# Stick-breaking attention and HGRN2 on one core: new durations in a list schedule, the causal mask by a matmul, softplus's maximum by ScalarE

## The chip, the core and the metric

The kernel runs on one core of a Trainium2 chip. The metric is device time in microseconds (us), of one launch; the time of a kernel is the median of its runs. A core has TensorE (PE, matmuls, with weight loads shown apart as PEld), VectorE (DVE), ScalarE (ACT), GpSimd (POOL) and SyncE (SP, which issues DMAs). Each engine takes its instructions strictly in the order in which they are written for it, and waits on semaphores for the others.

## The reference

One decoder block on 1024 tokens of width 1024, in float32: a norm and a projection to 5632 columns, two branches (8 heads of stick-breaking attention, 4 heads of HGRN2), a gated merge, a projection, and a SwiGLU network. The change lies in the attention:

```python
def stick_breaking_attention(q, k, v):
    ...
        z = jnp.einsum('bhtd,bhsd->bhts', qb, kb).astype(jnp.float32) * scale
        ...
        causal = s_idx < t_idx
        sp = jnp.where(causal, jax.nn.softplus(z), 0.0)
        rest = lax.cumsum(sp, axis=3, reverse=True) - sp
        w = jnp.where(causal, jnp.exp(jax.nn.log_sigmoid(z) - rest), 0.0)
```

The kernel uses log_sigmoid(z) = z - softplus(z): the weight is exp(z - c), with c the running sum of softplus from the right, the own column included. Softplus is max(z, 0) + ln(1 + exp(-|z|)). Where a key is not in the past, z is set to -2^100, which makes softplus and weight 0.

## The kernel before

All float32 factors are split into a high and a low part in TensorE's own 32-bit format, so a product is two or three matmuls. The program has three parts: stage one (projections, both branches), stage two (merge and output projection), and the SwiGLU network with Strassen-Winograd products. Only stage one is touched.

**Stage one's order is made by a planner.** Functions such as `proj`, `scores`, `values` and `hgrn` don't issue instructions; they record operations through helpers that give each a duration: `A` (ScalarE), `V` (VectorE), `G` (GpSimd), `M` and `T` (matmuls and transposes on TensorE) and `L` (loads and stores on SyncE, each charged at least 0.47 us, or its KB / 350). `Plan.issue` then plays a list schedule. It keeps a clock, adds fixed delays between engines (2.0 us behind a DMA), takes at each moment, per engine, the ready operation with the longest way to the end, and writes the instructions in that order. Tiles are counted in rings: an operation that needs a new tile waits until one of its ring is free. What stands in the program is thus a fixed order for each engine; how long things really take only decides where an engine then waits. All these instructions are issued from one line of `Plan.issue`, so they all have line L180 in the profile, and are told apart by the names of their tiles.

**Names of tiles.** `pj`: accumulators of the projections (3 banks); they have the lowest rank (-1) and so fill TensorE's holes. The last of them are 16 gate projections that nothing in the stage waits for. `oh`, `ol`: high and low part of a weight (split by GpSimd and VectorE). `hq`, `lq`, `hk`, `lk`: queries and keys of two heads, both parts. `qs`, `ks`: the layout for one head, with one buffer each (`ks0`, `ks1` for the two parts); six DMAs fill them. `z`: scores (2 banks). `aa`, `ww`: tiles of the softplus chain. `th`, `tl`: parts of a tile that is to be multiplied. `vv`: values. `ms`: other matmul results (3 banks). `kb`, `dl`, `ql`, `tail`, `state`: HGRN2.

**The score chain** (`scores`, line 548 on). For each of 4 pairs of heads, each head of it and each block of 128 queries, the scores of 128 to 1024 keys are made in one or two tiles of up to 512 columns; 96 tiles in all, 64 of them with a diagonal block. For a tile: two matmuls (queries by `ks0`, by `ks1`) into a bank `z`; on the diagonal VectorE overwrites the future with `never` under the mask `future`; ScalarE makes |z|, Exp and Ln; VectorE adds max(z, 0), scans from the right, and subtracts the scan from `z`; ScalarE takes Exp. The bank comes free with the subtraction.

```python
V(stt, aw, zw, 0.0, aw, n=w, op0=ALU.max, op1=ALU.add)
V(nc.vector.tensor_tensor_scan, cw[:, ::-1], aw[:, ::-1], aw[:, ::-1],
  0.0 if prev is None else prev[:, 0:1], op0=ALU.add, op1=ALU.max, n=w,
  aps=prev is not None)
```

The scan computes state = max(a + state, a), which is a + state since both are at least 0. `values` (line 589) transposes the weights, splits them and multiplies by `vv`; `hgrn` (line 637) runs the other branch.

Of the kernel before, what the change touches and what calls it, by code (L numbers as in the profile page):

```python
# [19 lines left out]
P = 128  # L20
# [7 lines left out]
NEG = -float(2.0**100)  # L28
# [172 lines left out]
def hybrid_block(ctx: ExitStack, tc, xT, wi, wb, wo, wg, wu, wd, vec, outT):  # L201
    nc = tc.nc
# [46 lines left out]
    bones_r = const1.tile([P, P], F32R, name="bones_r")  # L249
    future = const1.tile([P, P], I8, name="future")  # L250
    never = const1.tile([P, P], F32, name="never")
    eps_t = const.tile([P, 1], F32, name="eps_t")
# [10 lines left out]
    def setup(sp):  # L263
        make_identity(nc, ident)
        t2 = sp.tile([P, P], F32, tag="t2", name="t2")
        nc.vector.memset(t2, 0.0)
        nc.vector.memset(t2[0:64, 0:64], 1.0)
        nc.vector.memset(t2[64:128, 64:128], 1.0)
        nc.vector.tensor_copy(bones_r, t2)
        nc.vector.memset(never, NEG)  # L270
        nc.gpsimd.memset(future, 1.0)
        nc.gpsimd.affine_select(
            out=future, in_=future, pattern=[[1, P]], compare_op=ALU.is_ge, fill=0.0,
            base=0, channel_multiplier=-1)
        nc.vector.tensor_scalar(qg, vt[:, V_Q:V_Q + 1], 0.125, None, op0=ALU.mult)
# [12 lines left out]
        nc.vector.tensor_scalar(omlb, lb, -1.0, 1.0, op0=ALU.mult, op1=ALU.add)  # L288
        nc.vector.tensor_scalar(nomlb, omlb, -1.0, None, op0=ALU.mult)
# [34 lines left out]
    pre.close()  # L324
    future = future.bitcast(U8)

# [37 lines left out]
    def V(fn, *args, n=HALF, aps=0, rank=0, part=False, holds=(), **kw):  # L364
        us = 0.07 + n / 960 + 0.061 * aps
        return plan.op("V", us, [(fn, args, kw)], rank, part=part, holds=holds)

    def G(fn, *args, us, rank=0, after=(), holds=(), **kw):
        return plan.op("G", us, [(fn, args, kw)], rank, after, holds=holds)

    def M(cols, mms, rank=0, after=(), holds=()):

        return plan.op("P", cols / 2400 + 0.003 * len(mms),
                       [(nc.tensor.matmul, m[:3], dict(start=m[3], stop=m[4])) for m in mms],
                       rank, after, holds=holds)

    def T(outs, after=(), holds=()):

        return plan.op("P", 0.11 * len(outs), [(nc.tensor.transpose, (o, i, ident), {})
                                               for o, i in outs], 0, after, holds=holds)  # L380
# [19 lines left out]
    def pool_copy(dst, src, rank=0, after=(), holds=()):  # L400
        return G(nc.gpsimd.tensor_scalar, dst, src, 1.0, 0.0, op0=ALU.mult, op1=ALU.add, us=0.6,
                 rank=rank, after=after, holds=holds)
# [38 lines left out]
    def take_x(h):  # L441
# [47 lines left out]
    def sums(out, src, w, n, after=()):  # L489

        hi, lo = new("th", dt=F32R)[:, :n], new("tl", dt=F32R)[:, :n]
        G(nc.gpsimd.tensor_scalar, hi, src, 1.0, 0.0, op0=ALU.mult, op1=ALU.add,
          us=0.05 + n / 930, holds=(lo,) if after else (lo, out))
        V(tt, lo, src, hi.bitcast(F32), op=ALU.subtract, n=n)
        return M(2 * n, [(out, w, hi, True, False), (out, w, lo, False, True)], after=after)
# [52 lines left out]
    def scores(j, last):  # L548
        d = heads[j]
        for e in range(2):  # L550
# [9 lines left out]
            for tb in range(8):  # L560
                n = (tb + 1) * P
                prev = None
                for c0, c1 in [(0, n)] if n <= 512 else [(512, n), (0, 512)]:
# [73 lines left out]
    def hgrn(hd, last):  # L637
# [5 lines left out]
        for h in range(2):  # L643
# [7 lines left out]
            pair = lambda t, m: t.rearrange("p (n u m) -> p n u m", u=2, m=m)  # L651
            G(nc.gpsimd.tensor_tensor, at, key, q, op=ALU.mult, us=1.15, after=(last,))
            dg = new("ms")
# [3 lines left out]
            for li, m in enumerate(LEVELS):  # L657
                nb = HALF // (2 * m)
                bv = pair(bb, m)
                if m == 1:  # L660
# [4 lines left out]
                    for t, u in ((key, 0), (q, 1)):  # L665
                        G(nc.gpsimd.tensor_tensor, ev, ev, pair(t, 1)[:, :, u, :], op=ALU.mult,
                          us=0.6)
                    lv = new("ms")
# [37 lines left out]
            ds_ = new("ms")  # L706
            M(2048, [(ds_[:, c], ktok[:, c], vtok[:, c], True, True) for c in cs])
            before = []
# [15 lines left out]
            o, sq = new("tail"), new("tail")  # L724
            d["free hi", h] = M(4096, mms, holds=(o, sq))
            A(nc.scalar.copy, o, op, ps=True)
# [393 lines left out]
```

## Time and profile before

| | us |
|---|---|
| median of 3 runs | 1580.96 (1579.17 to 1581.63) |
| the profiled execution's own time | 1582.63 |
| its span (first to last instruction) | 1580.9 |
| last matmul of stage one that is no projection | starts at 692.2 |
| first matmul of stage two | after 742.5 |

Over the span TensorE is busy for 1531.5 us (97%), VectorE for 1223.1 (77%), ScalarE for 751.6 (48%) and GpSimd for 215.3 (14%). A busy TensorE is not one at its peak: matmuls overlap, and the ends that the profile shows are modelled. In a row of the profile "aa<-z" means that `aa` is written and `z` read; "x96" is a count; behind the bar follow busy time, mean duration in ns, and the idle time of the engine just before, with what ended it. Waits are given as total, number of times and longest.

### The profile page before, as it was taken

The page shows a single profiled execution, that of the slowest core. Times are in us where ns is not written, and L with a number is a line of the kernel's source. Part 1 is how long each engine was busy: PE and PEld are TensorE (multiplying, and loading weights), DVE is VectorE, ACT ScalarE, POOL GpSimd, SP SyncE. Part 2 cuts the span into 40 slices and gives each one's busy share as a digit, 9 for nine tenths or more (in the row PEclk, how much of TensorE's full clock was granted, in tenths as well). Part 3 has the DMA queues.
Part 4 walks back from the last instruction along what each step waited for, and adds up shares of the span by engine and source line. Part 5 has one row for each costly group of instructions (what it writes and reads, how often), then busy time and mean ns, then how long its engine had stood idle before and what let it go on. Part 6 is the DMA issues. An engine that isn't in the chain of part 4 may idle for free.

```text
span 1580.9 us, 20533 instructions
## 1 busy us (share of the span) xinstructions
PE 1531.5 (97%) x7213; PEld 1249.6 (79%) x7213; DVE 1223.1 (77%) x2095; ACT 751.6 (48%) x1375; POOL 215.3 (14%) x231
## 2 busy tenths in 40 slices
PE   7999999999999999999999999999999999999999
PEld 5778887887778778888888878788888888778887
DVE  8798889999999776962657799888887777566553
ACT  5555767577657655452333363333333333244442
POOL 6121202301121000322441210000000000000000
PEclk9999999999999999999999999999999999999999
DMA  4303132113312232154334454666643333687672
GB/s 165 88 29 89 62 77 69 39 55 78 92 34 67 74 92 59 54 198 141 121 121 128 150 157 169 213 213 213 213 160 107 107 107 107 234 276 220 195 221 94
DMA packets 82247, 201.12 MB, mean 127 GB/s; under 512 B 9824, under 2 KB 11872, under 8 KB 80736
## 3 DMA queue, kind: packets, MB, share of 16 engines
q1 hardware_dynamic: 77536, 191.42, 38.5%
q10 hardware_dynamic: 4608, 8.39, 1.5%
q8 instruction: 57, 0.93, 0.3%
q14 instruction: 46, 0.38, 0.1%
HBM read 131.61 MB, written 55.57 MB: 118 GB/s over the span
## 4 chain that ended last, share of the span: by engine, by line
PE 71%; DVE 15%; DMA 5%; ACT 4%; issue 3%; SPq 1%; POOL 1%; DVEq 0%; ACTq 0%; POOLq 0%
PE f L908 25%; PE pj L180 16%; PE ms L180 6%; DVE aa L180 4%; PE f L1054 4%; PE f L1056 4%; PE f L1052 4%; PE pj L300 2%; PE pj L299 2%; PE pj L301 2%; DMA ks<-lk 2%; ACT aa L180 2%; PE z L180 2%; DMA rb<-act_d 1%; DVE ol L180 1%
## 5 line engine op out<-in xcount | busy, mean ns | idle before, releaser
L180 PE MATMUL pj<-ah,oh 128*128 128x512 f32 x704 | 288.9, 410 | 1.2 <-POOL oh L180 1.2
L180 PE MATMUL pj<-ah,ol 128*128 128x512 f32 x704 | 278.1, 395 | 0.4 <-DVE ol L180 0.4
L180 PE MATMUL pj<-al,oh 128*128 128x512 f32 x704 | 277.2, 394 | 0.0
L908 PE MATMUL f<-fh,oh 128*128 128x512 f32 x616 | 243.9, 396 | 3.2 <-ACT p L962 1.7
L908 PE MATMUL f<-fl,oh 128*128 128x512 f32 x616 | 243.5, 395 | 0.6 <-DVE fl L838 0.6
L908 PE MATMUL f<-fh,ol 128*128 128x512 f32 x616 | 243.2, 395 | 0.0
L235 ACT CAST oh<-w 128x512 fp32r<-128x512 f32 x168 | 102.4, 620 | 191.6 <-PE f L908 145.9
L180 PEld LDWEIGHTS pj<-ah,ol 128*128 128x128 f32 x704 | 133.5, 190 | 31.1 <-DVE ol L180 1.3
L180 PEld LDWEIGHTS pj<-ah,oh 128*128 128x128 f32 x704 | 134.3, 191 | 24.5 <-POOL oh L180 2.2
L180 PEld LDWEIGHTS pj<-al,oh 128*128 128x128 f32 x704 | 134.3, 191 | 22.3 <-issue 0.2
L236 DVE TENSOR_TENSOR ol<-w,oh 128x512 fp32r<-128x512 f32 x168 | 113.8, 684 | 37.7 <-ACT oh L235 37.4
L908 PEld LDWEIGHTS f<-fh,oh 128*128 128x128 f32 x616 | 115.5, 188 | 33.5 <-ACT p L962 2.2
L908 PEld LDWEIGHTS f<-fl,oh 128*128 128x128 f32 x616 | 115.5, 188 | 28.7 <-DVE fl L838 1.0
L908 PEld LDWEIGHTS f<-fh,ol 128*128 128x128 f32 x616 | 115.5, 188 | 28.1
L180 POOL TENSOR_SCALAR oh<-w 128x512 fp32r<-128x512 f32 x84 | 66.0, 787 | 396.2 <-PE pj L180 326.4
L1052 PE MATMUL f<-bh,ah 128*128 128x512 f32 x296 | 115.3, 393 | 4.0 <-ACT bh L235 4.0
L1054 PE MATMUL f<-bl,ah 128*128 128x512 f32 x296 | 117.5, 397 | 1.3 <-DVE bl L236 1.3
L1056 PE MATMUL f<-bh,al 128*128 128x512 f32 x296 | 117.3, 396 | 0.0
L236 DVE TENSOR_TENSOR al<-ra,ah 128x512 fp32r<-128x512 f32 x73 | 50.4, 690 | 73.1 <-ACT ah L235 72.9
L180 DVE TENSOR_TENSOR_SCAN aa<-aa 128x384 f32<-128x384 f32 (+3 forms) x96 | 95.1, 992 | 1.1
L235 ACT CAST ah<-ra 128x512 fp32r<-128x512 f32 x73 | 45.5, 623 | 102.8 <-PE f L1054 95.3
L180 DVE TENSOR_TENSOR ol<-w,oh 128x512 fp32r<-128x512 f32 x84 | 62.0, 739 | 18.7 <-POOL oh L180 18.1
(272 smaller groups left out, 3015.1 us busy)
## 6 DMA issues: line engine op xcount, KB each, us to landing
w<-wi SPq DMA_DIRECT2D x42, 512.0 KB, 3.6
rb<-act_d SPq DMA_DIRECT2D x73, 256.0 KB, 4.0
w<-wg SPq DMA_DIRECT2D x22, 512.0 KB, 3.8
w<-wu SPq DMA_DIRECT2D x22, 512.0 KB, 4.1
w<-wd SPq DMA_DIRECT2D x22, 512.0 KB, 6.7
wd_d<-ds SPq DMA_DIRECT2D x44, 256.0 KB, 5.2
act_d<-c SPq DMA_DIRECT2D x11, 1024.0 KB, 3.9
act_d<-bs SPq DMA_DIRECT2D x44, 256.0 KB, 3.3
```

The costliest lines, as they stand in the source:

```text
L180: fn(*[a.real() if isinstance(a, View) else a for a in args], **{k: v.real() if isinstance(v, View) else v for k, v in kw.items()})
L235: pin(nc.scalar.copy(hi, src))
L236: pin(nc.vector.tensor_tensor(lo, src, hi.bitcast(F32), op=ALU.subtract))
L299: nc.tensor.matmul(out, hi[:, ws], a[ka][0][:, hs(h)], start=first and i == 0, stop=False)
L300: nc.tensor.matmul(out, hi[:, ws], a[ka][1][:, hs(h)], start=False, stop=False)
L301: nc.tensor.matmul(out, lo[:, ws], a[ka][0][:, hs(h)], start=False, stop=last and i == n - 1)
L908: nc.tensor.matmul(out, a[i][:, ws], bl[k][j], start=start and k == 0 and i + j == 0, stop=k == 3 and i == 1, skip_group_check=True)
L1052: nc.tensor.matmul(bank[d], hi[:, ws], bh, start=first and p == 0, stop=False, skip_group_check=True)
L1054: nc.tensor.matmul(bank[d], hi[:, ws], bl, start=False, stop=False, skip_group_check=True)
L1056: nc.tensor.matmul(bank[d], lo[:, ws], bh, start=False, stop=p == NP - 1, skip_group_check=True)
```

## The change

Four edits, all in stage one:

1. Durations that the planner uses: a scan costs two passes instead of one; matmuls 2255 columns per us instead of 2400; transposes, GpSimd's operations and HGRN2's small matmuls get new figures. Loads (`L`) and the delays between engines stay.
2. The mask: `never` now holds -2^100 on and above the diagonal and 0 below, and a third matmul, identity by `never`, adds it to the diagonal block between the two score matmuls. VectorE's overwriting goes.
3. Softplus's maximum: ScalarE makes Relu(z) in a second tile (`ww`, later overwritten with the weights), and VectorE's addition goes.
4. The scan adds that tile: state = (a + state) + Relu(z).

```diff
-    future = const1.tile([P, P], I8, name="future")
-    never = const1.tile([P, P], F32, name="never")
+    never = const1.tile([P, P], F32R, name="never")
+    ident_r = const1.tile([P, P], F32R, name="ident_r")
...
     def V(fn, *args, n=HALF, aps=0, rank=0, part=False, holds=(), **kw):
-        us = 0.07 + n / 960 + 0.061 * aps
+        cycles = 2 * n if fn == nc.vector.tensor_tensor_scan else n
+        us = 0.067 + cycles / 960 + 0.061 * aps
...
-        return plan.op("P", cols / 2400 + 0.003 * len(mms),
+        return plan.op("P", us or cols / 2255 + 0.003 * len(mms),
...
-        return plan.op("P", 0.11 * len(outs), [(nc.tensor.transpose, (o, i, ident), {})
+        return plan.op("P", 0.11 * len(outs) - 0.08, [(nc.tensor.transpose, (o, i, ident), {})
...
-            G(nc.gpsimd.tensor_tensor, acc, acc, sq, op=ALU.add, us=1.15, after=(last_split[0],))
+            G(nc.gpsimd.tensor_tensor, acc, acc, sq, op=ALU.add, us=1.5, after=(last_split[0],))
...
-        M(2048 * 2, [(ss, ones, acc, True, True)])
+        M(2048, [(ss, ones, acc, True, True)])
...
-                    last = M(2 * w, mms, after=(last,))
                     if diag:
-                        V(nc.vector.copy_predicated, z[:, w - P:w], future, never, n=P)
+                        mms.insert(1, (z[:, w - P:w], ident_r, never, False, False))
+                    last = M(2 * w + P * diag, mms, after=(last,))
                     a, c, y = new("aa"), new("aa"), new("ww")
                     aw, cw, yw = a[:, :w], c[:, :w], y[:, :w]
                     A(act, aw, zw, AF.Abs, n=w, ps=True)
+                    A(act, yw, zw, AF.Relu, n=w, ps=True)
                     A(act, aw, aw, AF.Exp, n=w, scale=-1.0)
                     A(act, aw, aw, AF.Ln, n=w, aps=1, bias=one_t)
-                    V(stt, aw, zw, 0.0, aw, n=w, op0=ALU.max, op1=ALU.add)
-                    V(nc.vector.tensor_tensor_scan, cw[:, ::-1], aw[:, ::-1], aw[:, ::-1],
-                      0.0 if prev is None else prev[:, 0:1], op0=ALU.add, op1=ALU.max, n=w,
+                    V(nc.vector.tensor_tensor_scan, cw[:, ::-1], aw[:, ::-1], yw[:, ::-1],
+                      0.0 if prev is None else prev[:, 0:1], op0=ALU.add, op1=ALU.add, n=w,
                       aps=prev is not None)
...
-                last = M(8 * (n + 64), [(lv[:n, c * 64:(c + 1) * 64], dl[:, c * P:c * P + n],
+                last = M(0, [(lv[:n, c * 64:(c + 1) * 64], dl[:, c * P:c * P + n],
                                          ql[:, c * 64:(c + 1) * 64], True, True)
-                                        for c in range(4)], after=(last,))
+                                        for c in range(4)], after=(last,),
+                         us=0.43 + 0.003 * n)
```

The new durations move instructions all over the stage. The first place that matters later is on TensorE, between the two heads of the second pair, where queries and keys are loaded anew. `z` by the numbered `ks` are the last scores of the old head and, at the end, the first of the new one; before:

```order
L180 MATMUL z<-ks_2200,qs 128x512
L180 MATMUL z<-ks_2218,qs 128x512
L180 MATMUL pj<-ah_158,oh 128x512
...
L180 MATMUL ms<-th,ones_r 128x512
L180 MATMUL ms<-tl,ones_r 128x512
L180 MATMUL pj<-ah_148,oh 128x512
...
L180 MATMUL ms<-ql,dl 64x64 x4
L180 MATMUL z<-ks_2796,qs 128x128
L180 MATMUL z<-ks_2817,qs 128x128
```

and after the change:

```order
L180 MATMUL z<-ks_2288,qs 128x512
L180 MATMUL z<-ks_2309,qs 128x512
L180 MATMUL pj<-ah_162,oh 128x512
...
L180 MATMUL ms<-th,vv 128x256
L180 MATMUL ms<-tl,vv 128x256
...
L180 MATMUL z<-ks_2784,qs 128x128
L180 MATMUL z<-never,ident_r 128x128
L180 MATMUL z<-ks_2799,qs 128x128
```

Between the old head's last score matmul and the new head's first stood 36 projection matmuls, 2 wide and 4 narrow others; now there are 27 projection matmuls and 4 others of 256 columns. The mask matmul stands between the two of a tile.

The second place is VectorE's queue in the middle of the scores (the scan is shown as the other operations with three operands are: `aa<-aa` before, `aa<-aa,ww` now; `ww<-z,aa` is the subtraction that frees the bank). Before:

```order
L180 COPY_PREDICATED z<-future,never 128x128
L180 TENSOR_TENSOR ol<-w,oh 128x512
L180 SCALAR_TENSOR_TENSOR aa<-z,aa 128x512
L180 SCALAR_TENSOR_TENSOR aa<-aa 128x512
L180 SCALAR_TENSOR_TENSOR aa<-z,aa 128x128
L180 TENSOR_TENSOR tl<-ms,th 128x512
L180 SCALAR_TENSOR_TENSOR aa<-aa 128x128
L180 TENSOR_TENSOR ww<-z,aa 128x512
```

and after the change:

```order
L180 SCALAR_TENSOR_TENSOR aa<-aa,ww 128x512
L180 TENSOR_TENSOR ol<-w,oh 128x512
L180 SCALAR_TENSOR_TENSOR aa<-aa,ww 128x384
L180 TENSOR_TENSOR ww<-z,aa 128x512
L180 TENSOR_TENSOR tl<-ms,th 128x384
L180 TENSOR_TENSOR ww<-z,aa 128x384
```

A tile with a diagonal took four instructions here (overwrite, addition, scan, subtraction) and takes two.

More of the change, by code (lines that the diff above doesn't have):

```diff
@@ L269, in setup @@
         nc.vector.tensor_copy(bones_r, t2)
-        nc.vector.memset(never, NEG)
-        nc.gpsimd.memset(future, 1.0)
+        nc.vector.tensor_copy(ident_r, ident)
+        t3 = sp.tile([P, P], F32, tag="t3", name="t3")
+        nc.gpsimd.memset(t3, NEG)
         nc.gpsimd.affine_select(
-            out=future, in_=future, pattern=[[1, P]], compare_op=ALU.is_ge, fill=0.0,
+            out=t3, in_=t3, pattern=[[1, P]], compare_op=ALU.is_ge, fill=0.0,
             base=0, channel_multiplier=-1)
+        nc.vector.tensor_copy(never, t3)
         nc.vector.tensor_scalar(qg, vt[:, V_Q:V_Q + 1], 0.125, None, op0=ALU.mult)
@@ L324, in hybrid_block @@
     pre.close()
-    future = future.bitcast(U8)
     warm = pm()
@@ L369, in G, with M @@
         return plan.op("G", us, [(fn, args, kw)], rank, after, holds=holds)
-    def M(cols, mms, rank=0, after=(), holds=()):
-        return plan.op("P", cols / 2400 + 0.003 * len(mms),
+    def M(cols, mms, rank=0, after=(), holds=(), us=None):
+        return plan.op("P", us or cols / 2255 + 0.003 * len(mms),
                        [(nc.tensor.matmul, m[:3], dict(start=m[3], stop=m[4])) for m in mms],
@@ L400, in pool_copy @@
     def pool_copy(dst, src, rank=0, after=(), holds=()):
-        return G(nc.gpsimd.tensor_scalar, dst, src, 1.0, 0.0, op0=ALU.mult, op1=ALU.add, us=0.6,
+        return G(nc.gpsimd.tensor_scalar, dst, src, 1.0, 0.0, op0=ALU.mult, op1=ALU.add, us=0.68,
                  rank=rank, after=after, holds=holds)
@@ L492, in sums @@
         G(nc.gpsimd.tensor_scalar, hi, src, 1.0, 0.0, op0=ALU.mult, op1=ALU.add,
-          us=0.05 + n / 930, holds=(lo,) if after else (lo, out))
+          us=0.07 + n / 840, holds=(lo,) if after else (lo, out))
         V(tt, lo, src, hi.bitcast(F32), op=ALU.subtract, n=n)
@@ L651, in hgrn @@
             pair = lambda t, m: t.rearrange("p (n u m) -> p n u m", u=2, m=m)
-            G(nc.gpsimd.tensor_tensor, at, key, q, op=ALU.mult, us=1.15, after=(last,))
+            G(nc.gpsimd.tensor_tensor, at, key, q, op=ALU.mult, us=1.3, after=(last,))
             dg = new("ms")
@@ L666, in hgrn @@
                         G(nc.gpsimd.tensor_tensor, ev, ev, pair(t, 1)[:, :, u, :], op=ALU.mult,
-                          us=0.6)
+                          us=1.0)
                     lv = new("ms")
@@ L706, in hgrn @@
             ds_ = new("ms")
-            M(2048, [(ds_[:, c], ktok[:, c], vtok[:, c], True, True) for c in cs])
+            M(0, [(ds_[:, c], ktok[:, c], vtok[:, c], True, True) for c in cs], us=0.86)
             before = []
@@ L724, in hgrn @@
             o, sq = new("tail"), new("tail")
-            d["free hi", h] = M(4096, mms, holds=(o, sq))
+            d["free hi", h] = M(0, mms, holds=(o, sq), us=0.215 * len(mms))
             A(nc.scalar.copy, o, op, ps=True)
```

## The prediction

> **What bounds the kernel now.** I read the windows view first, to see what each engine does in the stretches of the first stage; then TensorE's waits in that stage; then the timeline around single waits. The windows view gives, for each stretch, busy time and count of TensorE (PE), its weight loads, VectorE (DVE), ScalarE (ACT) and GpSimd, then TensorE's granted clock, DMA share and GB/s.
>
> ```profile
> 45.00:200.00 155.00, 148.25 (x767) 123.17 (x767) 133.80 (x260) 94.13 (x189) 29.10 (x35) 0.98 0.25 67
> 200.00:500.00 300.00, 286.60 (x1574) 238.12 (x1573) 283.20 (x541) 204.81 (x408) 56.40 (x65) 0.99 0.24 61
> 500.00:692.00 192.00, 185.01 (x985) 153.53 (x985) 149.81 (x284) 109.49 (x218) 27.21 (x35) 0.98 0.27 76
> 692.00:743.00 51.00, 51.00 (x226) 42.21 (x225) 18.76 (x19) 21.82 (x28) 16.42 (x14) 1.00 0.58 205
> ```
>
> TensorE sets the end of the stage: from 692 us on it does nothing but projections (`pj`) that wait for nobody, and those are filler that could have stood in any earlier hole. So every microsecond in which TensorE stood still before 692 us is a microsecond of the stage, and a microsecond saved there is saved in the whole. The rows also show who is second: VectorE, 133.8 + 283.2 + 149.8 = 566.8 of 647 us (88%), and 94% between 200 and 500 us. What TensorE waited for, up to 743 us (total, times, longest), first by its matmuls, then by its weight loads:
>
> ```profile
> PE z L180 <- DMA ks<-lk: 12.2, 6, 2.4
> PE z L180 <- DVE ww L180: 5.2, 12, 0.8
> PE ms L180 <- DVE tl L180: 3.3, 4, 1.3
> PE ms L180 <- DVE dl L180: 2.0, 2, 1.2
> PE ms L180 <- DVE kb L180: 1.6, 4, 0.6
> PE z L180 <- DVE tl L180: 1.1, 1, 1.1
> ```
> ```profile
> PEld z L180 <- DVE ww L180: 15.6, 32, 1.2
> PEld ms L180 <- DVE tl L180: 7.9, 14, 1.6
> PEld ms L180 <- DVE kb L180: 2.9, 5, 0.9
> PEld z L180 <- DVE tl L180: 1.4, 1, 1.4
> ```
>
> Two causes, then: VectorE that is late (5.2 + 3.3 + 2.0 + 1.6 + 1.1 = 13.2 us in 23 waits by the matmul rows), and keys on their way (12.2 us in 6). The matmul rows understate. A row's end is modelled: its mean is 389 ns, yet the 223 matmuls of the last stretch take 50.35 us, 226 ns each, so each wait hides some 0.16 us.
>
> ```profile
> 692.59:742.94 50.35, 50.35 (x223) 41.69 (x223) 18.76 (x19) 21.76 (x28) 16.42 (x14) 1.00 0.57 203
> ...
> L180 PE MATMUL pj<-al,oh 128*128 128x512 f32 x74 | 28.8, 389 | 0.0
> ```
>
> With 23 × 0.16 = 3.7 the VectorE waits come to 17 us; the weight-load rows, which see short waits too but also idle time that cost nothing, give 15.6 + 7.9 + 2.9 + 1.4 = 27.8. I take 20, nearer to the lower. The key waits become 13.2.
>
> **The change, part by part.** *VectorE loses work.* Gone are the 64 masking copies and the 96 additions of the maximum; the scan stays one scan (it read one tile twice, it now reads two).
>
> ```profile
> L180 DVE SCALAR_TENSOR_TENSOR aa<-z,aa 128x384 f32<-128x384 f32 (+3 forms) x96 | 52.6, 549 | 13.5 <-ACT aa L180 12.8
> L180 DVE COPY_PREDICATED z<-future,never 128x128 f32<-128x128 uint8 x64 | 19.7, 311 | 21.1 <-PE z L180 20.9
> L180 DVE TENSOR_TENSOR_SCAN aa<-aa 128x384 f32<-128x384 f32 (+3 forms) x96 | 95.1, 992 | 1.1
> L180 ACT ACTIVATE aa<-z 128x384 f32<-128x384 f32 (+3 forms) x96 | 46.1, 487 | 32.2 <-DVE z L180 28.9 <-PE z L180 2.4 <-PE pj L180 0.4
> ```
>
> That is 72.3 us, so VectorE falls to 494.5 of 647 us (76%). The chain from a score bank's matmul to its release loses one copy (0.31) and one addition (0.55 on average). The wait for that release averages 5.2 / 12 + 0.16 = 0.6 us, so most of those waits should go. The waits for `tl`, `dl` and `kb` are VectorE's queue being late behind scans: the scan's mean is 992 ns, and the old planner charged a scan as one pass, 0.07 + n/960, 0.60 us at 512 columns; the new one doubles the slope. Of the 20 us I let 16 go (at least 5, if the waits mostly find new places; at most all 20). For the scan's second tile I charge nothing: it took two operands before, both from one tile.
>
> *ScalarE gains 96 Relus* shaped like the Abs in the row above: 46 us. It was busy 94.1 + 204.8 + 109.5 = 408 of 647 us, so 454 (70%) after; Relu is needed by the scan alone and may stand behind Exp and Ln. Hidden: 0. Were ScalarE as full as VectorE was, each would lengthen the chain by its 0.49 us.
>
> *TensorE gains 64 mask matmuls* of 128 columns, each between two matmuls with other weights. None is in the trace; the nearest rows are two matmuls of 128 columns that follow each other with different weights:
>
> ```profile
> 592.34 0.22 PE L180 MATMUL ms<-th,vv 128*128 128x128 f32 x1
> 592.40 0.28 PE L180 MATMUL ms<-tl,vv 128*128 128x128 f32 x1
> 592.52 0.44 PE L180 MATMUL pj<-ah,oh 128*128 128x512 f32 x1
> ```
>
> From start to start 0.06 and 0.12 us. Eight masks stand in the first tile after new keys, where TensorE waits anyway; 56 × 0.09 = +5.0 us (56 × 0.06 = 3.4 to 64 × 0.12 = 7.7). The Trainium skill ("TensorE: Matmul & The Clock Gate", LDWEIGHTS) gives a weight load of 128 columns as 128/1.2 = 107 ns; by that estimate the term would be 6.8 and the sum 1.8 higher.
>
> *The reloads of queries and keys get less cover.* Each head's half loads `qs` and both `ks` into the only buffers, after the last old score matmul. One case, TensorE's rows and the issues on SyncE (start, duration):
>
> ```profile
> 203.35 0.62 PE L180 MATMUL z<-ks,qs 128*128 128x512 f32 x2
> ...
> 211.37 0.22 PE L180 MATMUL z<-ks,qs 128*128 128x128 f32 x1
> 213.87 0.45 PE L180 MATMUL z<-ks,qs 128*128 128x128 f32 x1 [2.27 <-DMA ks<-lk]
> ```
> ```profile
> 204.06 0.48 SPq L180 DMA_DIRECT2D qs<-hq  x1
> 204.58 0.60 SPq L180 DMA_DIRECT2D qs<-lq  x1
> 205.67 1.55 SPq L180 DMA_DIRECT2D ks<-hk  x2
> 207.32 2.51 SPq L180 DMA_DIRECT2D ks<-lk  x2
> ```
>
> From the old pair to the second new matmul 213.87 - 203.35 = 10.5 us pass; the work between gave 7.5. Neither planner knows this: for both a load costs 0.73 us and 2.0 us of delay, 6 × 0.73 + 2.0 = 6.4. The lines for it are not changed. I counted the matmuls that the written order puts between the last old and the first new score matmul, at 0.23 us for 512 columns, 0.12 for 256 and 0.11 for a transposed 128. Before, the seven reloads behind the first have 7.0, 7.5, 9.0, 7.4, 12.2, 14.5 and 8.9 us; after, 6.5, 27.8, 6.7, 6.9, 7.3, 8.7 and 6.9. The old planner took TensorE as faster than it is, which made covers long by mistake. Missing from 10.5: before 3.5 + 3.0 + 1.5 + 3.1 + 0 + 1.6 = 12.7, after 4.0 + 3.8 + 3.6 + 3.2 + 1.8 + 3.6 = 20.0 (left out is the one in each whose new keys come late from their own projection, about 2.5; so is the first reload, 2.5). That makes 17.7 against 25.0. The trace has 13.2 where I count 17.7, since other waits lie inside the covers; scaled, 7.3 × 13.2 / 17.7 = +5 us (0, if other waits fill the gap, to 25.0 - 13.2 = +12).
>
> *The clock.* After key waits the granted clock falls to half for one stretch of 3.41 us:
>
> ```profile
> 60.01:63.42 3.41, 3.41 (x11) 2.73 (x11) 2.86 (x8) 2.57 (x8) 0.00 (x0) 0.50 0.21 84
> 131.69:135.10 3.41, 3.40 (x9) 2.73 (x10) 1.89 (x5) 0.99 (x3) 0.00 (x0) 0.50 0.02 7
> 213.61:217.02 3.41, 3.15 (x12) 2.99 (x13) 1.68 (x3) 1.88 (x5) 0.00 (x0) 0.50 0.37 142
> 517.40:520.81 3.41, 3.25 (x12) 2.86 (x13) 0.50 (x2) 0.93 (x4) 0.00 (x0) 0.50 0.51 169
> 568.60:572.01 3.41, 3.41 (x18) 3.41 (x17) 2.71 (x8) 2.44 (x7) 0.00 (x0) 0.50 0.00 0
> 368.50:371.91 3.41, 3.31 (x20) 2.95 (x21) 2.68 (x7) 2.35 (x7) 0.88 (x1) 1.00 0.00 0
> ```
>
> Five of six waits did it, at 1.7 us each; the sixth, near 366 us, did not. Longer and more waits: one stretch more, +1.7 (three fewer, -5, to three more, +5). The Trainium skill (same page, Part 1) has the clock halve after at least one idle window of about 3.4 us. The trace is stricter: a wait of 2.27 us at 211 us was enough. By the rule's letter this term would be 0 and the time 1.7 lower.
>
> *The ends of the stage.* The new constants cost VectorE two casts instead of a memset at the start, where it then idles 0.68 us for a DMA: 0. After the last other matmul, 171 projections (39 us) follow instead of 223 (50). Stage two needs its operands, whose last split ended 24 us after 692:
>
> ```profile
> 2.62 0.15 DVE L275 TENSOR_SCALAR qg<-vt 128x1 f32<-128x1 f32 x1 [0.68 <-DMA vt<-vec]
> ...
> 712.99 3.45 DVE L781 TENSOR_TENSOR ol<-o,oh 128x1024 fp32r<-128x1024 f32 x2
> ```
>
> 39 covers 24, so 0; only if that chain grew by over 15 us would stage two start late.
>
> **Sum:** -16 + 5.0 + 5 + 1.7 = -4.3 us. The profiled execution took 1582.6 us (span 1580.9), the median is 1581.0; the difference is carried to the median: 1576.7, say 1577.
>
> **The rivals.** *The whole gain*: all 20 us of VectorE waits go, masks cost 3.4, and what still waits inside the covers keeps the reloads as they are: -16.6, 1564. For it: with work counted as above, a score bank is asked for again less than 1 us after its chain (summed from the rows' durations) 28 times before and 8 times after. Against it: covers of 6.5 to 7.3 us against 10.5 needed.
>
> *The reloads take it back (slower).* The place is the second score matmul after each reload. Price: all 11.8 us of uncovered time and all eight reloads with half a clock, +5: with -16 and +5.0, +5.8, 1587. It decides from the point where reload waits and half clocks grow by more than 16 - 5 = 11 us. For it: six of the seven new covers are at the planner's own minimum. Against it: some other waits will stay inside them.
>
> *The waits only move.* A written order stalls wherever anything is later than planned, and with honest durations the plan is tighter. Then 5 us go instead of 16, the rest stands: +6.7, 1588. Against it: VectorE has 72 us less to do and 24% of the stretch free.
>
> **How the numbers follow.** Forecast 1577, 0.42 (its own range 1571 to 1583); the whole gain 0.24; reloads 0.24; waits move 0.10. The range reaches to both outer groups, 1563 to 1589. This kernel's measurement can't tell 0.2%, 3.2 us, from no change, so faster means under 1577.8 and slower over 1584.1. Faster: 0.24 of the forecast's 0.42 and all of the whole gain, 0.48. Same: 0.16 of the forecast, 0.04 of the reloads, 0.02 of the waits that move, 0.22. Slower: the rest, 0.30.
>
> **What would show it.** Right: VectorE near 495 us between 45 and 692 us; the waits of `z` for `ww` under 2 us where they were 5.2, those for `tl`, `dl` and `kb` at half; the wait for `ks` up to 17 us in seven or eight places, each about 3 us, with six stretches at half clock; mask matmuls 0.06 to 0.12 us apart from their neighbours. Wrong: VectorE waits over 10 us in sum (they moved), or key waits at or under 12 us (covers held), or a stage two that starts with a wait.

## The result and the profile after

The change makes the kernel **slower**: 1592.91 us (median of 8 runs, 1587.0 to 1599.63) against 1580.07 us before (8 runs, 1576.75 to 1582.93). The ratio is 1.0086, with a 95% interval from 1.0069 to 1.0104. Forecast were 1577 us and a range of 1563 to 1589; neither holds. The profiled execution of the change took 1590.11 us (span 1588.4, mean granted clock 0.989).

All of it is lost in stage one. Its last projection starts at 750.2 us where it was 742.5, and what follows takes 1588.4 - 750.2 = 838.2 us where it took 1580.9 - 742.5 = 838.4. The last matmul that is no projection has moved from 692.2 to 712.1 us. The windows view of the changed kernel (columns as in the prediction: length, then busy time and count of PE, PEld, DVE, ACT, POOL, then granted clock, DMA share, GB/s):

```profile
45.00:200.00 155.00, 147.14 (x787) 123.60 (x786) 124.28 (x226) 107.93 (x224) 27.29 (x33) 0.98 0.26 68
200.00:500.00 300.00, 287.82 (x1550) 241.33 (x1549) 237.28 (x434) 194.57 (x401) 54.82 (x67) 0.99 0.23 61
500.00:712.00 212.00, 200.39 (x1103) 168.37 (x1102) 149.63 (x265) 139.35 (x286) 33.95 (x37) 0.98 0.25 71
712.00:750.50 38.50, 38.50 (x174) 31.92 (x173) 16.20 (x16) 19.64 (x25) 13.12 (x12) 1.00 0.73 254
45.00:692.00 647.00, 615.35 (x3322) 516.12 (x3321) 499.66 (x905) 431.28 (x891) 114.81 (x134) 0.98 0.25 66
```

VectorE is relieved as the change intends: 499.66 us of the 647 between 45 and 692 us, against 566.8. TensorE gains nothing from it: 615.35 us busy there, against 148.25 + 286.60 + 185.01 = 619.9. What it waits for up to the end of the stage (total, times, longest) says why:

```profile
PE z L180 <- DMA ks<-lk: 20.3, 8, 4.6
PE ms L180 <- DVE tl L180: 4.8, 5, 2.0
PE ms L180 <- DVE tail L180: 3.1, 2, 2.7
PE ms L180 <- DVE kb L180: 3.0, 3, 2.4
PE z L180 <- DVE ww L180: 2.6, 5, 1.5
...
PE ms L180 <- DVE dl L180: 0.2, 1, 0.2
```

The wait for new keys has grown from 12.2 us in 6 places to 20.3 in 8. The wait for a score bank (`z` for `ww`) has halved and the one for `dl` is nearly gone, but those for `tl` and `kb` are longer. One of the eight key waits, in the timeline of TensorE (start, duration):

```profile
432.63 0.62 PE L180 MATMUL z<-ks,qs 128*128 128x512 f32 x2
...
440.52 0.22 PE L180 MATMUL z<-ks,qs 128*128 128x128 f32 x1
440.58 0.27 PE L180 MATMUL z<-never,ident_r 128*128 128x128 f32 x1
443.89 0.30 PE L180 MATMUL z<-ks,qs 128*128 128x128 f32 x1 [3.04 <-DMA ks<-lk]
```

From the last old pair to the second new score matmul 11.3 us pass; the work between them ends 3 us early. The mask starts 0.06 us behind its predecessor.

**Where the 7.7 us of the profiled stage come from.** I took, for neighbouring matmuls, the distance from start to start less the usual one of that shape, and sorted the excess by what released the second. In us, before and after: keys 13.2 and 22.6 (+9.4); VectorE, from 45 us on, 20.4 and 14.0 (-6.4); `tail` in the first 45 us 6.7 and 3.4 (-3.2); matmuls at half clock 11.6 and 14.1 (+2.5). With 5.6 for the masks, measured below, the sum is +7.9. The medians differ by more, 12.8 us, because the change's runs spread more: over its eight runs the mean granted clock goes from 0.990 in the one of 1587.0 us to 0.982 in the one of 1599.6.

### The profile page after: what moved, and what is told of

The parts are those of the page before. It is cut to its first block, busy times and chain, and to the rows that moved or that the text cites. A ratio compares the mean times of both kernels' runs of the same rounds, so it can differ in the third digit from the quotient of the medians.

```text
span 1588.4 us, 20588 instructions
## 1 busy us (share of the span) xinstructions
PE 1534.6 (97%) x7277; PEld 1257.1 (79%) x7277; DVE 1166.0 (73%) x1936; ACT 782.6 (49%) x1471; POOL 214.9 (14%) x231
## 4 chain that ended last, share of the span: by engine, by line
PE 74%; DVE 12%; DMA 7%; issue 3%; SPq 2%; ACT 2%; POOL 1%; DVEq 0%; POOLq 0%; ACTq 0%
PE pj L180 22%; PE f L911 19%; PE ms L180 8%; PE f L1057 4%; PE f L1059 4%; PE f L1055 4%; DMA ks<-lk 3%; PE z L180 3%; PE pj L302 2%; PE pj L301 2%; PE pj L303 2%; SPq L180 2%; DMA w<-wu 1%; DVE ol L236 1%; DVE aa L180 1%
## 5 line engine op out<-in xcount | busy, mean ns | idle before, releaser
L236 DVE TENSOR_TENSOR ol<-w,oh 128x512 fp32r<-128x512 f32 x168 | 115.0, 691 | 36.4 <-ACT oh L235 36.1
L180 DVE TENSOR_TENSOR_SCAN aa<-aa,ww 128x512 f32<-128x512 f32 (+3 forms) x96 | 95.0, 1009 | 29.5 <-ACT aa L180 18.9
L180 PE MATMUL z<-ks,qs 128*128 128x128 f32 (+3 forms) x192 | 58.2, 373 | 23.6 <-DMA ks<-lk 20.3
```

Of the source, the lines that this page charges most:

```text
L180: fn(*[a.real() if isinstance(a, View) else a for a in args], **{k: v.real() if isinstance(v, View) else v for k, v in kw.items()})
L236: pin(nc.vector.tensor_tensor(lo, src, hi.bitcast(F32), op=ALU.subtract))
```

## The experiments

Four theories stood at first: the reloads have lost their cover; the mask matmuls cost more than they look; ScalarE's Relu holds up the scans; the new durations make a worse order by themselves. Each kernel ran beside the kernel before on the same chip, whose median there was 1577.4 to 1579.0 us; ratios are to that.

### Each half of the change alone

Edits 2 to 4 with the planner's old durations (against the change; all durations are set back, two are shown):

```diff
-        cycles = 2 * n if fn == nc.vector.tensor_tensor_scan else n
-        us = 0.067 + cycles / 960 + 0.061 * aps
+        us = 0.07 + n / 960 + 0.061 * aps
...
-        return plan.op("P", us or cols / 2255 + 0.003 * len(mms),
+        return plan.op("P", cols / 2400 + 0.003 * len(mms),
```

> The change with its durations undone: mask matmul, Relu and the scan's second tile stay, the planner charges what it charged before. Theory R (time is lost at the reloads of queries and keys, because the new order puts less TensorE work behind the last old scores): the written order has 6.7, 17.8, 7.4, 7.0, 7.3, 7.6 and 8.8 us of work there (before 7.0, 7.5, 9.0, 7.4, 12.2, 14.5, 8.9; the change 6.5, 27.8, 6.7, 6.9, 7.3, 8.7, 6.9), so the key waits should be near 18 us, between before (12.2) and the change (20.3), and the time between 1580 and 1592. Theory D (the new durations are to blame): VectorE has 72 us less to do and the old covers come back; 1565 to 1575. Theory M (the mask matmuls cost much more than 5 us): as slow as the change, 1590 or more, with key waits as before.

Measured: 1595.50 us, 1.009 (1.007 to 1.011). The other half, the new durations with mask and maximum on VectorE as before:

```diff
-                        mms.insert(1, (z[:, w - P:w], ident_r, never, False, False))
-                    last = M(2 * w + P * diag, mms, after=(last,))
+                    last = M(2 * w, mms, after=(last,))
+                    if diag:
+                        V(nc.vector.copy_predicated, z[:, w - P:w], future, never, n=P)
...
-                    A(act, yw, zw, AF.Relu, n=w, ps=True)
...
+                    V(stt, aw, zw, 0.0, aw, n=w, op0=ALU.max, op1=ALU.add)
```

> The durations alone: the planner charges the new figures, the instructions are those of before (mask and maximum on VectorE). Theory R: the order has 5.4, 7.0, 4.6, 7.2, 7.5, 8.5 and 7.0 us of work at the reloads, less than the change; key waits over 20 us, and VectorE waits of before or fewer, so 1585 to 1595. Theory M: without mask matmuls no slower than before, 1575 to 1582.

Measured: 1608.57 us, 1.018 (1.0158 to 1.0201), the slowest of all and more than any theory had expected. TensorE's waits, first with the old durations, then with the new ones alone:

```profile
PE z L180 <- DMA ks<-lk: 13.6, 7, 2.6
PE z L180 <- DVE ww L180: 7.6, 17, 1.1
...
PE z L180 <- DMA o_d<-ot: 3.1, 1, 3.1
```
```profile
PE z L180 <- DMA ks<-lk: 18.1, 8, 3.1
PE ms L180 <- DVE kb L180: 9.2, 8, 5.0
PE z L180 <- DMA ks<-hk: 3.0, 5, 1.1
```

The durations fall as the sole cause: with the old durations edits 2 to 4 lose as much as the change. Both halves lose alone, and both have key waits above the 12.2 us of before. With the old durations they are 13.6 us, less than the 18 that theory R expected. The one wait put down to a store (`o_d<-ot`) also stands at the first new score matmul after a reload, though; with its 3.1 us the sum is 16.7. The time lies 3.5 us above theory R's range. Theory M fits this run about as well; the run without masks, below, settles it. New durations without the lighter VectorE lose most. There the keys cost 21.1 us, the waits for `kb` come on top, and from 45 us on the profile has sixteen cells of 3.41 us at half clock, where before has five (a stretch at half clock lasts one such cell or several).

### What the planner charges for a reload

The planner charges a load its KB / 350, so 0.73 us for each of the six. I raised that number alone, in the two calls that load `qs` and `ks`; the transfers themselves stay as they are. First to 1.28 us (448):

```diff
-                                d["q"][i][64 * e:64 * e + 64].bitcast(F32), 256, part=True)
+                                d["q"][i][64 * e:64 * e + 64].bitcast(F32), 448, part=True)
...
-                                    d["k"][i][64 * e:64 * e + 64].bitcast(F32), 256, part=True)
+                                    d["k"][i][64 * e:64 * e + 64].bitcast(F32), 448, part=True)
```

> The change, and the planner charges each of the six loads of a reload 1.28 us instead of 0.73 (448 KB in place of 256 in its figure; what is loaded stays). The order then has 8.2, 11.8, 8.1, 12.2, 9.8, 10.7 and 10.7 us of work at the reloads. Theory R: key waits fall from 20.3 us to 8 to 10, most half-clock stretches behind them go, and the time falls by 10 to 18 us against the change: 1573 to 1582, with runs that differ less from each other. Theory M or W (waits only move): 1588 or more; the key waits go and others grow.

Measured: 1572.50 us (1570.18 to 1573.53), 0.995 (0.9933 to 0.9966). The change with nothing but another planner's charge is 20 us faster, and now faster than the kernel before. Its waits for banks and keys:

```profile
PE z L180 <- DVE ww L180: 8.7, 8, 5.2
...
PE z L180 <- DMA ks<-lk: 0.8, 1, 0.8
```

The key waits are gone (0.8 us of 20.3): the theory of the reloads holds. In their place stands one wait of 5.2 us for a bank. Its timeline in this kernel (start, duration), on ScalarE, on VectorE, and TensorE's next score matmul:

```profile
257.41 0.58 ACT L180 ACTIVATE aa<-z 128x512 f32<-128x512 f32 x1
...
258.69 0.72 ACT L180 ACTIVATE aa<-aa,one_t 128x512 f32<-128x512 f32 x1
260.53 0.63 ACT L180 ACTIVATE tmp<-xg 128x512 f32<-128x512 f32 x1 [1.12 <-DVE xg L180]
...
263.94 0.63 ACT L180 ACTIVATE dl<-dl 128x512 f32<-128x512 f32 x1 [0.98 <-DVE dl L180]
264.48 1.06 ACT L180 ACTIVATE ww<-z 128x512 f32<-128x512 f32 x2
...
265.05 0.41 DVE L180 TENSOR_TENSOR ql<-xq,dl 128x256 f32<-128x256 f32 x1
265.38 1.20 DVE L180 TENSOR_TENSOR_SCAN aa<-aa,ww 128x512 f32<-128x512 f32 x1
...
268.65 1.28 DVE L180 TENSOR_TENSOR_SCAN aa<-aa,ww 128x512 f32<-128x512 f32 x1
...
270.16 0.68 DVE L180 TENSOR_TENSOR ww<-z,aa 128x512 f32<-128x512 f32 x1
...
270.90 1.22 PE L180 MATMUL z<-ks,qs 128*128 128x512 f32 x2 [5.24 <-DVE ww L180]
```

An Abs starts at 257.41 and an Ln at 258.69, but two Relus stand behind other work in ScalarE's fixed order, which itself waited twice for VectorE, and start at 264.48. The first scan follows at 265.38. VectorE did not stand still for the Relu: from 255.75 to 266.6 us it was busy without a gap, with work that its order puts ahead of the scan. The same order puts the second scan and other work ahead of the subtraction at 270.16, and TensorE's wait ends with that subtraction. So this wait comes from VectorE's written order. No scan can be planned ahead of its Relu, so the late Relus may be why the planner put the scans there; that was not tried for this place.

The same charge in the kernel before:

> The kernel before, and the planner charges each load of a reload 1.28 us, as in the run that did this to the change (1572.5 us against 1579.0 before). Work at the reloads by the order: 12.1, 12.5, 12.0, 9.1, 9.2, 11.1, 10.6 us. Theory R (the reload's wait is a matter of its cover, whatever else is in the kernel): key waits fall from 12.2 us to about 3, and 8 to 14 us are gained on before: 1565 to 1571; the change then adds nothing on top of it. Theory E (the edits are worth something once the reloads are covered): VectorE's waits of before stay, 1574 to 1579.

Measured: 1564.84 us, 0.9912 (0.9899 to 0.9925). No key wait is left in its list. So the missing cover was a fault of the kernel before too, worth 13 to 15 us in this order, which the change made larger.

### The masks themselves

The 64 mask matmuls are planned and not issued, so the order stays the change's; future keys are then not masked.

```diff
-                       [(nc.tensor.matmul, m[:3], dict(start=m[3], stop=m[4])) for m in mms],
+                       [(nc.tensor.matmul, m[:3], dict(start=m[3], stop=m[4])) for m in mms
+                        if m[1] is not ident_r],
```

> The change without its 64 mask matmuls, everything else and every engine's order kept (future keys are then not masked; the output is another). It measures the masks' own price. Theory R: 3 to 7 us faster than the change (56 x 0.06 to 0.12, and the eight masks at the reloads for nothing). Theory M: over 10 us faster.

Measured: 1587.30 us (12 runs), 1.0048 (1.0029 to 1.0066). The masks cost 1592.9 - 1587.3 = 5.6 us, and without them the kernel is still slower than before. By the ratios to the kernel before, 0.0038 of 1580, they cost 6.0 us, give or take 4 by the two intervals. They are a part of the loss, of about the size that was forecast, and not what made the forecast miss.

### More charge, and the edits one by one

The change with 1.46 us for a load (512 in the diff above):

> The change with the reload's loads charged 1.46 us each (512 KB in place of 448). Work at the reloads: 10.2, 13.9, 11.8, 11.9, 10.7, 11.6, 11.8 us, all at about the 10.5 that a reload takes. With 1.28 it was 1572.5 us and the key waits were 0.8 us, so theory R expects no more gain from the reloads, 1569 to 1576. If still more of the time hangs on them (half-clock stretches), 1565 or less.

Measured: 1557.15 us (1555.47 to 1559.29), 0.9866 (0.9852 to 0.988), 15 us better than with 1.28, where no gain was expected. The same two waits, and the row of its scans (behind the bar: busy time, mean ns, idle time before them and what ended it):

```profile
PE z L180 <- DVE ww L180: 4.3, 7, 1.1
...
PE z L180 <- DMA ks<-lk: 0.2, 1, 0.2
```
```profile
L180 DVE TENSOR_TENSOR_SCAN aa<-aa,ww 128x512 f32<-128x512 f32 (+3 forms) x96 | 97.3, 1027 | 37.3 <-ACT aa L180 21.2 <-ACT ww L180 16.0
```

The 5.2 us wait is gone, though scans wait for Relu (`ACT ww`, 16.0 us) more than in the change (10.5, below): a scan that is late is dear only where TensorE has nothing else to do. With 1.28 us, mask and maximum were put back on VectorE singly:

> The change with the reload charged 1.28 us a load and the mask back on VectorE (the overwriting copy; Relu and the scan's second tile stay). TensorE saves the mask matmuls, which a run put at 5.6 us (1592.9 to 1587.3); VectorE gets 19.7 us back. If VectorE's relief is what pays: slower than 1572.5 by 2 to 6, up to 1579. If the matmul costs more than the relief: faster, 1566 to 1571.

> The change with the reload charged 1.28 us a load and softplus's maximum back on VectorE (no Relu; the mask matmul stays). VectorE gets 52.6 us back, ScalarE is rid of 46. If VectorE's relief pays: slower than 1572.5 by 5 to 12 (1577 to 1585), with VectorE waits over 20 us; one reload has only 4.7 us of work, worth 6 us of key wait and a half clock. If it doesn't: 1572 to 1577.

Measured: 1564.35 us with the old mask, 0.9907 (0.9893 to 0.9922); 1569.13 us with the old maximum, 0.9937 (0.992 to 0.9954). Both are faster than any of the ranges set for them. By these two each edit costs, 8 and 3 us; the 3 are within what the runs spread. Then all of it with 1.46 us: the kernel before, the new durations alone, the old mask, the old maximum.

> The kernel before, with each load of a reload charged 1.46 us in the plan (1.28 gave 1564.8). Work at the reloads by the order: 12.0, 13.4, 9.6, 12.1, 11.6, 11.7, 11.5 us. With the same charge the change took 1557.2. If the change's edits are worth something once reloads are covered: 1560 to 1570, slower than 1557.2. If they are not: 1553 to 1558.

> The new durations alone (mask and maximum on VectorE), each load of a reload charged 1.46 us. Without the charge the durations alone took 1608.6, the worst of all. Theory R: most of that was reloads, so 1562 to 1575; two reloads still have little work (8.9 and 5.4 us). If the durations themselves make a bad order: 1580 or more.

> The change with each load of a reload charged 1.46 us and the mask back on VectorE; with the mask matmul it took 1557.2. With a charge of 1.28 the mask on VectorE was the faster one (1564.4 against 1572.5). If the matmul's 5.6 us are the larger price: 1550 to 1556. If VectorE's 19.7 us are: 1559 to 1566. One reload has only 7.9 us of work.

> The change with each load of a reload charged 1.46 us and the maximum back on VectorE (mask matmul kept); with Relu on ScalarE it took 1557.2. If VectorE's 52.6 us pay: 1562 to 1572. If the Relu, which the order puts behind other work on ScalarE so that the scan waits for it, takes back what VectorE saves: 1553 to 1560. Two reloads have only 8.7 and 7.4 us of work.

| | 1.28 us | 1.46 us |
|---|---|---|
| before | 1564.8 | 1574.4 |
| new durations alone | not run | 1575.5 |
| change, mask on VectorE | 1564.4 | 1571.2 |
| change, maximum on VectorE | 1569.1 | 1559.8 |
| change | 1572.5 | 1557.2 |

The ratios at 1.46 us are, from the top, 0.9976 (0.9964 to 0.9987), 0.9983 (0.997 to 0.9997), 0.9961 (0.9946 to 0.9975), 0.9882 (0.9863 to 0.9902) and the 0.9866 above. Three of the four (1574.4, 1575.5 and 1571.2 us) fell outside every range set for them; only the old maximum came out where one was, that of a late Relu that takes back what VectorE saves. The sign of the mask flips between the columns: by matmul it costs 8 us in one and gains 14 in the other. The maximum's goes from 3 us lost to 3 gained, neither clear of noise. In none of these kernels do key waits pass 1.7 us, so it is no longer the reloads. The kernel before at 1.46 us has one long wait of its own:

```profile
PE ms L180 <- DVE kb L180: 8.0, 6, 4.9
PE z L180 <- DVE ww L180: 7.3, 11, 1.8
```

It had 1.6 us for `kb` at 1.28. Behind the long wait stand five cells of 3.41 us at half clock, six in all from 45 us on, where the profile at 1.28 has none there. One wait of some 5 us at one place in the written order, and the half clock behind it, is worth as much as an edit.

### Is that chance of the order?

Two more charges, 1.37 (480) and 1.55 us (544), for both kernels:

> The kernel before, each load of a reload charged 1.37 us (480 KB). With 1.28 and 1.46 it took 1564.8 and 1574.4, so one small step of a charge moves it by 10 us. If that is chance of the written order, this one falls anywhere in 1562 to 1577; work at the reloads 9.0, 11.5, 12.9, 11.1, 11.5, 13.2, 11.0 us.

> The change, each load of a reload charged 1.37 us; with 1.28 and 1.46 it took 1572.5 and 1557.2. Theory E (the edits are worth about 5 us once the reloads are covered, with some 8 us of chance on top): below its partner with the same charge, 1557 to 1570. Theory N (they are worth nothing): 1562 to 1577, on either side.

> The kernel before, each load of a reload charged 1.55 us (544 KB). Work at the reloads 11.6, 12.3, 8.9, 5.5, 11.4, 13.9, 13.9 us: one short by 5 us and one by 1.6, so 1568 to 1580.

> The change, each load of a reload charged 1.55 us. Work at the reloads 11.1, 13.9, 8.0, 13.8, 10.2, 13.9, 12.3 us. Theory E: 1556 to 1568 and below its partner; theory N: 1562 to 1577.

| charge of a load, us | 0.73 | 1.28 | 1.37 | 1.46 | 1.55 | mean of the last four |
|---|---|---|---|---|---|---|
| before | 1580.1 | 1564.8 | 1565.8 | 1574.4 | 1578.5 | 1570.9 |
| change | 1592.9 | 1572.5 | 1561.4 | 1557.2 | 1566.0 | 1564.2 |

The new ratios are 0.9922 (0.99 to 0.9944), 0.9893 (0.987 to 0.9915), 0.9998 (0.9983 to 1.0013) and 0.9921 (0.9899 to 0.9943). A step of 0.09 us in one charge, which changes no instruction but only their order, moves a kernel by 1 to 11 us. Against that the edits are worth 6.7 us on the mean of four charges, and 7.7 between the best of each. Theory E holds at both new charges, but at 1.28 the change is the slower one. Four orders with gains from -7.7 to 17.2 us are few: that the edits gain at all is likely, not shown, and the size stays open. Part of the chance is the clock: in the order of the table the profiles have 5, 0, 2, 6 and 4 cells at half clock from 45 us on before, and 6, 4, 3, 1 and 3 after the change, each worth up to 1.7 us.

### Relu first

What the late Relu costs, by an order in which a tile's Exp may not be planned ahead of its Relu, in the change, and then with 1.46 us for a load as well:

```diff
-                    A(act, yw, zw, AF.Relu, n=w, ps=True)
-                    A(act, aw, aw, AF.Exp, n=w, scale=-1.0)
+                    relu = A(act, yw, zw, AF.Relu, n=w, ps=True)
+                    A(act, aw, aw, AF.Exp, n=w, scale=-1.0, after=(relu,))
```

> The change, with each tile's Relu put ahead of its Exp on ScalarE (Exp depends on it in the plan). Work at the reloads stays short: 6.0, 8.1, 6.9, 6.8, 6.0, 8.8, 7.1 us. Theory L (late Relus hold the scans, and that is why VectorE's waits fell so little): the 10.5 us that scans waited for the Relu tile go, and TensorE's waits for VectorE fall by 3 to 6 us; the time stays over 1583 because of the reloads. Otherwise: the scans wait as long, for Ln instead, and TensorE's waits for VectorE are as before.

> The same with each load of a reload charged 1.46 us, where the change took 1557.2. Work at the reloads 12.3, 12.1, 11.9, 12.8, 11.2, 11.5, 11.6 us, all covered. Theory L: 1552 to 1557. Otherwise 1557 to 1566.

Measured: 1590.90 us, 1.0075 (1.0051 to 1.0099), and 1553.72 us (1553.48 to 1554.61), 0.9838 (0.9819 to 0.9857). In the first, TensorE's waits and the scans' row:

```profile
PE z L180 <- DMA ks<-lk: 20.7, 8, 4.1
...
PE ms L180 <- DVE tl L180: 3.3, 6, 1.4
...
PE ms L180 <- DVE kb L180: 1.9, 2, 1.2
...
PE z L180 <- DVE ww L180: 0.4, 2, 0.3
```
```profile
L180 DVE TENSOR_TENSOR_SCAN aa<-aa,ww 128x512 f32<-128x512 f32 (+3 forms) x96 | 95.2, 1007 | 54.6 <-ACT aa L180 54.4
```

No scan waits for Relu any more. Scans now stand still longer for Ln, 54.6 us in all against 29.5, and yet TensorE's waits for VectorE fall to 3.3 + 1.9 + 0.4 + 0.2 (`dl`) = 5.8 us from 10.6. (It is another order, too, so not all of that need be Relu's.) The time gains only 2 us, less than either set of runs spreads: the key waits stay at 20.7, and from 45 us on its profile has ten cells at half clock where the change has six. With the reloads covered as well it is the **fastest kernel here**, 25 us under the kernel before on the same chip (1578.9). It is 3.4 us under the change at the same charge, which the intervals of the two ratios don't quite separate. Its window, and its wait for keys:

```profile
45.00:692.00 647.00, 637.93 (x3494) 536.33 (x3493) 516.60 (x934) 450.35 (x923) 120.53 (x143) 1.00 0.28 79
```
```profile
PE z L180 <- DMA ks<-lk: 1.3, 1, 1.3
```

TensorE is busy for 637.93 of these 647 us, 18 to 23 us more than in either kernel, and never at half clock there. The stage's last projection starts at 717.9 us.

## Why the prediction was wrong

**VectorE's waits: the relief came, most of the waits stayed.** VectorE's work fell to 499.66 us (494.5 forecast), the banks' waits from 5.2 to 2.6 us (under 2 forecast). The 20 us that I set for all of its waits are right, 20.4 by the starts. The step that failed is "Of the 20 us I let 16 go": 6.4 went, near the 5 of the rival "the waits only move", and the waits named in the prediction still come to 4.8 + 3.0 + 2.6 + 0.2 = 10.6 us, just over the 10 that were to show it wrong. A part of that is ScalarE's step: "Relu is needed by the scan alone and may stand behind Exp and Ln. Hidden: 0." Relu took the 46 us that I gave it, but the scan now needs both, and ahead of 12 of the 96 scans VectorE stood still for the Relu. Rows of the changed kernel:

```profile
L180 DVE TENSOR_TENSOR_SCAN aa<-aa,ww 128x512 f32<-128x512 f32 (+3 forms) x96 | 95.0, 1009 | 29.5 <-ACT aa L180 18.9 <-ACT ww L180 10.5
L180 ACT ACTIVATE ww<-z 128x128 f32<-128x128 f32 (+3 forms) x96 | 45.2, 488 | 6.2 <-PE ms L180 6.0
```

Before, VectorE stood still 1.1 us ahead of its scans and 13.5 ahead of the additions, which took the wait for Ln; now it is 29.5 ahead of the scans, 10.5 of it for Relu. Idle time of VectorE is no loss by itself, as the order with Relu first shows. What speaks for the Relu's place is TensorE's waits for VectorE (`ww`, `tl`, `dl` and `kb`) at equal charge. Relu first brings them from 10.6 to 5.8 us, and with 1.46 us a load from 10.0 to 6.8. The maximum back on VectorE, 52.6 us of work, hardly moves them: 13.1 against 14.4 with 1.28 us, 11.2 against 10.0 with 1.46. So with late Relus, taking the maximum from VectorE bought TensorE next to nothing, and some 3 to 5 of the missing 9.6 us go with the Relu's place, as far as pairs of orders can show it. The cause of the rest stays open. A share of busy time (70% of ScalarE) had been read as cover; it says nothing of where in the queue the instruction stands. The scan's second tile costs nothing, as forecast: 95.0 us against 95.1.

**The reloads: the mechanism was named, its price too low.** Forecast +5 (0 to +12); measured +8.1 by the waits, +9.4 by the starts, eight places as counted. The count from the written order was good: 25.0 us of missing cover, of which 22.6 show. The scaling was not: before, 13.2 of the counted 17.7 showed, and I carried that share over. Why more of it shows after the change was not tried; fewer of VectorE's waits now lie inside the covers, which would do it. The rival "reloads take it back", 1587, had the right story and needed the VectorE term to fail too: with 6.4 us in place of its 16, its sum is +15.4; the medians give +12.8.

**The masks:** +5.0 forecast, 5.6 measured. **The ends of the stage:** the end costs 0, as forecast. At the start 3.2 us were gained on `tail`, which I hadn't counted; an order made anew moves waits everywhere.

**The clock:** +1.7 forecast for one stretch more, and one more it is: from 45 us on the profiled run has six cells of 3.41 us at half clock where before had five. Two of the six stand together, behind the key wait of 4.6 us. Ahead of 45 us there are three where there were two, so matmuls at half clock cost 2.5 us more in all. Other runs have more, by their granted clock: the median of the change lies 2.8 us above its profiled run, while the profiled run of before, 1582.63, lies 2.6 above its median. Those 5.4 us and the 7.5 between the profiled runs are the 12.8 between the medians. The spread, 12.6 us over eight runs where before has 6.2, should have been part of the range, since long waits were forecast.

**The sum.** -4.3 forecast, +12.8 measured in the medians. In the order of their size: VectorE's term 9.6 too good, the reloads 4.4 too low, and the clock too low, by 0.8 in the profiled runs and by some 6 if what the medians add is put down to it, as the spread of the granted clock suggests; the masks 0.6; against these the start's 3.2. The sign hung on the first. The range ended at 1589 because each rival let only one term go wrong.

## What to carry to other kernels

In a list schedule, look first for the operation whose planned time is furthest from what the trace shows, and correct that one before judging an edit: here six loads were charged 0.73 us each and took 1.3, and that one number was worth 1.5 to 15 us to the kernel before and 20 to 36 to the changed one, against 6.7 for all four edits. Work that goes to an idle engine is hidden only if its place in that engine's queue is early enough; make it a dependency if the next operation needs it. And time an edit to such a kernel under several orders, since one order alone can turn its sign, as it did for the mask here.

## What the hardware showed that was not expected

**When the clock halves.** The prediction said that a wait of about 2.3 us is enough. The stretches at half clock lie on a fixed grid of 3.413 us, and what mostly decides is how long TensorE was busy in one cell of that grid. Cells of the changed kernel, a key wait of 1.89 us that was followed by half clock and, later, one of 2.28 that was not:

```profile
106.99:110.40 3.41, 1.59 (x13) 1.35 (x11) 3.10 (x9) 1.00 (x2) 0.00 (x0) 1.00 0.95 190
110.40:113.81 3.41, 3.33 (x13) 2.97 (x14) 0.76 (x2) 2.47 (x6) 0.00 (x0) 0.50 0.42 155
362.98:366.39 3.41, 2.68 (x14) 1.82 (x12) 3.41 (x5) 2.43 (x5) 0.66 (x1) 1.00 0.98 197
366.39:369.80 3.41, 1.74 (x8) 1.53 (x9) 1.12 (x3) 1.37 (x5) 0.16 (x1) 1.00 0.37 90
369.80:373.22 3.42, 3.42 (x20) 2.91 (x20) 3.40 (x8) 2.58 (x7) 0.46 (x1) 1.00 0.32 65
```

The first wait lies in one cell, which is left with 1.59 us of work; the other is split by the grid into cells with 2.68 and 1.74. A key wait of 2.92 us near 607 us, split into cells with 1.87 and 2.00, had no half clock behind it either. Over the profiles of all twenty kernels, from 45 to 720 us, all 41 cells at full clock with less than 1.5 us of work were followed by half clock, none with more than 2.3 was, and of the 84 between them 22 were: the limit lies near half a cell and is not sharp by this count, in which the ends of matmuls are modelled. Why a stretch sometimes lasts several cells is not explained by it. The Trainium skill ("TensorE: Matmul & The Clock Gate", Part 1) gives the same free-running window of 3413 ns, but has the clock halve after at least one idle window; here windows with up to 1.5 us of work were always enough. Since the grid doesn't follow the program, a wait of 2 to 3 us sometimes costs a stretch and sometimes doesn't; that this makes the runs spread (12.6 us in the change, 1.1 in the fastest kernel, whose profile has no stretch from 45 us on) fits, but was not tried apart.

**Six loads on one queue** of 256 KB each, between tiles of the core, land about 1.3 us apart: in the changed kernel one set is issued from 358.34 us and lands at 361.4, 362.6, 363.9, 365.2, 366.6 and 367.9. The sixth is 9.6 us behind the first issue, whereas a charge of 6 × 0.73 + 2.0 planned 6.4; 1.28 us each gives 9.7, which is the first of the charges tried that left no key wait of note.
